# A hybrid encoder layer on one core: the edge columns of group two's row tiles are written by an entry of the convolution's queue

## The chip, the cores and the metric

The kernel runs on one core of one Trainium2 chip. The core has five engines that work side by side, each through its own list of instructions in order, and that wait for one another on semaphores: TensorE (PE in the profile; its weight loads stand as PEld), VectorE (DVE), ScalarE (ACT), GpSimd (POOL) and SyncE (SP), which here only issues transfers. The metric is device time of one execution, in microseconds (us), lower is better. Each kernel is executed several times and the median is compared.

## The reference

One layer of an encoder on two groups of requests, 1024 rows and 256 rows, with shared weights:

```python
hn = rms_norm(x, norm_g)
proj = hn @ w_in
xbc, z_ssd, dt_raw, q, k, v, z_att, mq, z_mem = split_cols(proj, IN_SIZES)
xbc = jax.nn.silu(centred_dwconv(xbc, conv_w, conv_b))
xs, Bm, Cm = split_cols(xbc, (SSD_WIDTH, SSD_GROUPS * SSD_STATE, SSD_GROUPS * SSD_STATE))
```

`xs`, `Bm` and `Cm` feed a state-space scan in both directions, `q`, `k`, `v` an attention in a window of 128 rows, `mq` an attention on a memory of 256 rows. The three results are gated, joined and multiplied by `w_out`, and `x` is added.

The part that matters here is the convolution: each of the 1536 channels of `xbc` is convolved along the rows with five taps centred on the row (two rows to each side, zeros outside the request), a bias is added and SiLU taken. A block of rows therefore needs two rows from each neighbour, and where a request begins or ends it needs zeros.

## The kernel before

**Rows and channels.** The 1280 rows (1024 of the first request, then 256 of the second) are worked on in two groups of 640. For `xbc` the product is laid with channels on the 128 partitions and rows along the free axis, so that the convolution runs along the free axis. There are 12 such tiles of channels for each group. All products are in fp32 as three passes (high by high, low by high, high by low halves). A weight tile is loaded by SP (`wraw`), its high half is copied by ACT (`wh`, L206) and its low half subtracted by DVE (`wl`, L207); the two are called a split below.

**Group one** gets its `xbc` in the stretch before 500 us by another path (`ev_seven`). While it does so, it keeps the last four input columns of each channel tile in `carry` (L361).

**Group two** gets its `xbc` in six blocks, x0 to x5, in the stretch from 590 to 816 us. `block_feat` makes one block: 8 weight tiles, two tiles of channels (the pair), two halves of 320 rows, four accumulators in PSUM of the five in the pool `acc`. For each weight tile but the seventh it runs the matmuls; the seventh's are run with the eighth's. Behind the last matmul of the first channel tile comes its evacuation, behind the last one of the second its own. A block has 192 matmuls of 320 columns (L293, L294, L295), and 16 places (yields) at which other work is let in: two behind each of the first six weight tiles, four behind the eighth, after the first evacuation and ahead of the second.

**The row tile.** The evacuation of group two, the function `f` in `ev_conv` (L388), takes a tile `u` of 650 columns from the two buffers of tag `evu`. Columns 4 to 323 and 324 to 387 are the rest of the first request, 392 to 647 the second request; ACT copies these from PSUM (L394, L395, L396). The edge columns are written by DVE: 0 to 3 from `carry` (L391), 388 to 391 and 648 to 649 with zeros (L392, L393). The evacuation stands in a block of raised priority (`tc.high_priority(offset=HP[1])`, 100): the scheduler that lays each engine's instructions in order may place them earlier than where the program calls them. In the trace the edges of the first tile start at 601.54 us and its copies on ACT at 615.55.

**The queue of the convolution.** When the second tile of a pair is evacuated, `conv_two` makes a list of entries that is put into the queue `left`; one entry is taken at each of the 16 places of the next block (`one_left`, which calls `some_left`). An entry's instructions are put behind the latest weight split on ACT and DVE (`issue_after(marks)`), at ordinary priority. For one tile the entries are `first_tap` (ACT, L357, takes a `c` of tag `evt`, two buffers), four taps (DVE, L362), `silu` (ACT, L365), `last` (DVE, L368, which writes the finished rows into `u`; then SP stores them in two transfers, L372 and L373, into `xbc_d`). `conv_two` overlaps the two tiles by two entries, so a pair has 12. Behind x5 they run in the places of the block for `k`, `v` and `dt` (`block_tok`, one place behind each of 16 weight tiles, 15 matmuls each).

With 12 entries, the pairs of entries behind weight tiles 1 to 6 are: first tap and tap 1; taps 2 and 3; tap 4 with the second tile's first tap, silu with its tap 1; last, and its tap 2; its taps 3 and 4; its silu and its last. The four places behind the eighth weight tile are empty.

**What runs beside it.** At the same 16 places, `pump` takes steps of two more lists of work: the attentions (`attn`, `mem_attn`) and the scan (`ssd_up`). They use PSUM from a pool of three banks (`mix`). In `attn`, `scores` has TensorE write a score tile `psc` (L689, L690) that DVE reads (L691).

Of the kernel before, what the change touches and what calls it, by code (L numbers as in the profile page):

```python
# [44 lines left out]
def hymba_encoder_kernel(  # L45
# [7 lines left out]
    V, A, G, T, S = nc.vector, nc.scalar, nc.gpsimd, nc.tensor, nc.sync  # L53
# [23 lines left out]
    def const(shape, name, dtype=F32):  # L77
        return cp.tile(shape, dtype, tag=name, name=name)
# [22 lines left out]
    carry = const([P, 12, 4], "carry")  # L101
# [239 lines left out]
    left = deque()  # L341
# [7 lines left out]
    def conv_work(grp, fc, u):  # L349

        n = 646 if grp else 638
        cw = [vec[:, R_CW + k * 12 + fc:R_CW + k * 12 + fc + 1] for k in range(5)]
        c = []

        def first_tap():
            c.append(ev.tile([P, 650], F32, tag="evt", name="c")[:, :n])
            A.activation(c[0], u[:, :n], AF.Identity, scale=cw[0], bias=vec[:, R_CB + fc:R_CB + fc + 1])  # L357

        def tap(k):
            if grp == 0 and k == 2:  # L360
                V.tensor_copy(carry[:, fc, :], u[:, 638:642])  # L361
            V.scalar_tensor_tensor(out=c[0], in0=u[:, k:k + n], scalar=cw[k], in1=c[0], op0=ALU.mult, op1=ALU.add)  # L362

        def silu():
            A.activation(u[:, :n], c[0], AF.Tanh)  # L365

        def last():
            V.scalar_tensor_tensor(out=u[:, :n], in0=u[:, :n], scalar=1.0, in1=c[0], op0=ALU.add, op1=ALU.mult)  # L368
            if grp == 0:
                S.dma_start(xbc_d[fc, :, 0:638], u[:, :638])  # L370
            else:
                S.dma_start(xbc_d[fc, :, 638:1024], u[:, :386])  # L372
                S.dma_start(xbc_d[fc, :, 1024:1280], u[:, 390:646])  # L373
        return [first_tap] + [lambda k=k: tap(k) for k in range(1, 5)] + [silu, last]

    def conv_two(a, b):

        def both(f, g):
            def h():
                f()  # L380
                g()
            return h
        return a[:4] + [both(a[4], b[0]), both(a[5], b[1]), a[6]] + b[2:]

    def ev_conv(grp, f0):
        us = []

        def f(fc, ps):  # L388
            fc = f0 + fc
            u = ev.tile([P, 650], F32, tag="evu", name="u")  # L390
            V.tensor_copy(u[:, 0:4], carry[:, fc, :])  # L391
            V.memset(u[:, 388:392], 0.0)  # L392
            V.memset(u[:, 648:650], 0.0)  # L393
            A.activation(u[:, 4:324], ps[0][:, :320], AF.Copy)  # L394
            A.activation(u[:, 324:388], ps[1][:, :64], AF.Copy)  # L395
            A.activation(u[:, 392:648], ps[1][:, 64:320], AF.Copy)  # L396
            us.append(u)
            if len(us) == 2:
                left.extend(conv_two(*[conv_work(grp, f0 + i, us[i]) for i in range(2)]))
        return f  # L400

# [1257 lines left out]
    for b in range(6):  # L1659
        feat("x", b, ev_conv(1, 2 * b), 1, extra=one_left)  # L1660
# [120 lines left out]
```

## Time and profile before

| | |
|---|---|
| median of three runs | 1777.37 us (1776.67 to 1778.53) |
| the profiled execution | 1777.93 us, span from its first to its last instruction 1776.2 us |
| busy in the span: PE, PEld | 1763.4 us (99%), 1608.4 us (91%) |
| DVE, ACT, POOL | 1245.6 us (70%), 918.9 us (52%), 554.6 us (31%) |
| blocks x0 to x5, starts of the first matmuls | 590.2, 621.2, 658.0, 696.2, 735.9, 774.5 us |
| edge instructions L391, L392, L393 | 12 of each, 0.166, 0.062, 0.060 us (medians) |
| DVE idle in front of L391 | 4.9 us in all, 4 times, until stores into `xbc_d` landed |

An engine's busy time leaves out its waits. A wait is put down to the semaphore that came last. A start is counted from the first instruction of the span. Line numbers are those of the kernel before.

### The profile page before, as it was taken

Reading aid. Unit: us, or ns where it says so; the run is one execution under the profiler, and the core shown is the slowest. Engines: PE = TensorE matmul, PEld = TensorE weight load, DVE = VectorE, ACT = ScalarE, POOL = GpSimd, SP = SyncE. Lnnn points to the kernel's source line nnn. Section 1 sums busy time; section 2 is a strip of 40 time slices with the busy share of each in tenths; the row PEclk is TensorE's granted clock in tenths of the full one; section 3 lists DMA queues with packets and bytes.
Section 4 is the critical chain, followed back from the end, with each engine's and each line's share of the span. In section 5 each row is a group of like instructions: output and inputs, shape, how many; then the busy total and the mean of one; then the engine's idle time right before and its main releaser. Section 6 shows DMA issues by size and latency. Waiting matters only on the chain. (4 is left out here: it accounts for less than half of the span.)

```text
span 1776.2 us, 31998 instructions
## 1 busy us (share of the span) xinstructions
PE 1763.4 (99%) x11046; PEld 1608.4 (91%) x11046; DVE 1245.6 (70%) x2348; ACT 918.9 (52%) x2049; POOL 554.6 (31%) x980
## 2 busy tenths in 40 slices
PE   9999999999999999999999999999999999999999
PEld 7888999999998999999889988888988888899999
DVE  5595788888858878777765676557777654766665
ACT  5554555555434766656454565545446633543332
POOL 0105798998810100001000100011110000058775
PEclk9999999999999999999999999999999999999999
DMA  8653444445447544453635645557787854644442
GB/s 293 200 184 115 146 149 147 141 145 168 122 138 213 189 138 134 148 169 99 193 116 187 186 157 156 168 167 249 220 247 233 254 189 145 219 146 146 146 143 78
DMA packets 208210, 301.16 MB, mean 170 GB/s; under 512 B 19568, under 2 KB 86192, under 8 KB 208048
## 3 DMA queue, kind: packets, MB, share of 16 engines
q1 hardware_dynamic: 207904, 299.06, 54.5%
q8 instruction: 87, 1.43, 0.3%
q14 instruction: 75, 0.61, 0.1%
q10 hardware_dynamic: 144, 0.06, 0.0%
HBM read 236.36 MB, written 62.69 MB: 168 GB/s over the span
## 5 line engine op out<-in xcount | busy, mean ns | idle before, releaser
L207 DVE TENSOR_TENSOR wl<-wraw,wh 128x512 fp32r<-128x512 f32 (+1 forms) x480 | 346.7, 724 | 227.6 <-ACT wh L206 218.7
L206 ACT ACTIVATE wh<-wraw 128x512 fp32r<-128x512 f32 (+1 forms) x480 | 292.2, 613 | 294.3 <-PE acc L260 155.8
L258 PE MATMUL acc<-wh,xH 128*128 128x512 f32 (+1 forms) x1088 | 418.5, 385 | 0.6 <-DVE v_all L337 0.3
L260 PE MATMUL acc<-wh,xL 128*128 128x512 f32 (+1 forms) x1088 | 410.2, 377 | 0.0
L259 PE MATMUL acc<-wl,xH 128*128 128x512 f32 (+1 forms) x1088 | 409.8, 377 | 0.1
L258 PEld LDWEIGHTS acc<-wh,xH 128*128 128x128 f32 x1088 | 204.1, 188 | 37.6 <-issue 2.7
L260 PEld LDWEIGHTS acc<-wh,xL 128*128 128x128 f32 x1088 | 204.2, 188 | 36.8 <-issue 0.2
L259 PEld LDWEIGHTS acc<-wl,xH 128*128 128x128 f32 x1088 | 204.4, 188 | 35.7 <-issue 1.2
L293 PE MATMUL acc<-xH,wh 128*128 128x320 f32 x640 | 202.8, 317 | 0.0
L206 ACT ACTIVATE sh<-ws 128x384 fp32r<-128x384 f32 x176 | 91.3, 523 | 207.6 <-POOL ws L1256 109.6
L294 PE MATMUL acc<-xL,wh 128*128 128x320 f32 x640 | 198.6, 310 | 0.0
L295 PE MATMUL acc<-xH,wl 128*128 128x320 f32 x640 | 198.4, 310 | 0.0
L207 DVE TENSOR_TENSOR sl<-ws,sh 128x384 fp32r<-128x384 f32 x176 | 124.9, 713 | 98.1 <-ACT sh L206 94.5
L1256 POOL TENSOR_TENSOR ws<-wraw 128x128 f32<-128x128 f32 x176 | 112.9, 641 | 206.4 <-DMA wraw<-in_w_in_pairs_dram 86.3
L293 PEld LDWEIGHTS acc<-xH,wh 128*128 128x128 f32 x640 | 120.1, 188 | 2.6 <-issue 2.1
L294 PEld LDWEIGHTS acc<-xL,wh 128*128 128x128 f32 x640 | 120.2, 188 | 1.5 <-issue 1.2
L1256 POOL TENSOR_TENSOR ws<-wraw,ws 128x128 f32<-128x128 f32 x176 | 116.7, 663 | 13.8
L295 PEld LDWEIGHTS acc<-xH,wl 128*128 128x128 f32 x640 | 120.2, 188 | 0.7 <-issue 0.7
L1256 POOL TENSOR_TENSOR ws<-ws,wraw 128x128 f32<-128x128 f32 x176 | 118.2, 672 | 0.0
L1256 POOL TENSOR_TENSOR wraw<-wraw 128x128 f32<-128x128 f32 x176 | 111.6, 634 | 13.7
L635 POOL MEMSET lgw<- 128x1 f32 x40 | 3.9, 98 | 313.8 <-DVE lg L698 188.1
L362 DVE SCALAR_TENSOR_TENSOR c<-u,vec,c 128x638 f32<-128x638 f32 (+1 forms) x96 | 90.0, 939 | 9.9 <-ACT c L357 9.5
(440 smaller groups left out, 3954.1 us busy)
## 6 DMA issues: line engine op xcount, KB each, us to landing
wraw<-in_w_in_laid_dram SPq DMA_DIRECT2D x176, 256.0 KB, 2.9
wraw<-in_w_in_pairs_dram SPq DMA_DIRECT2D x112, 256.0 KB, 2.7
wraw<-in_w_out_laid_dram SPq DMA_DIRECT2D x64, 256.0 KB, 3.5
wraw<-in_w_out_pairs_dram SPq DMA_DIRECT2D x64, 256.0 KB, 2.7
rf<-ac SPq DMA_DIRECT2D x40, 256.0 KB, 4.1
rb<-ac SPq DMA_DIRECT2D x40, 256.0 KB, 4.7
wraw<-in_w_mem_laid_dram SPq DMA_DIRECT2D x32, 256.0 KB, 4.5
xst<-in_x_sample_dram SPq DMA_DIRECT2D x20, 256.0 KB, 5.0
```

What stands on the lines that cost most here:

```text
L206: a = A.activation(h, raw, AF.Copy)
L207: b = V.tensor_sub(l, raw, h.bitcast(F32))
L258: T.matmul(ps[t][:, :n], sh, h[:, :n], start=(k_ == 0), stop=False)
L259: T.matmul(ps[t][:, :n], sh, l[:, :n], start=False, stop=False)
L260: T.matmul(ps[t][:, :n], sl, h[:, :n], start=False, stop=(k_ == KT - 1))
L293: T.matmul(o, sh, cur["H", q][:, m, c], start=(k == 0), stop=False)
L294: T.matmul(o, sh, cur["L", q][:, m, c], start=False, stop=False)
L295: T.matmul(o, sl, cur["H", q][:, m, c], start=False, stop=(k == KT - 1))
L362: V.scalar_tensor_tensor(out=c[0], in0=u[:, k:k + n], scalar=cw[k], in1=c[0], op0=ALU.mult, op1=ALU.add)
L635: G.memset(w.bitcast(F32)[(slice(None),) + tuple(slice(n - 1, n) for n in shape)], 0.0)
L1256: G.tensor_tensor(out=o, in0=x, in1=y, op=op)
```

## The change

The three instructions that write a row tile's edge columns leave the evacuation and become a function `edges`. A new first entry of the queue calls it for both tiles of the pair; the entries of `conv_two` follow. A pair now has 13 entries for the 16 places. The instructions themselves, their number and their engine stay.

```diff
+    def edges(fc, u):
+        V.tensor_copy(u[:, 0:4], carry[:, fc, :])
+        V.memset(u[:, 388:392], 0.0)
+        V.memset(u[:, 648:650], 0.0)
+
     def ev_conv(grp, f0):
         us = []
 
         def f(fc, ps):
             fc = f0 + fc
             u = ev.tile([P, 650], F32, tag="evu", name="u")
-            V.tensor_copy(u[:, 0:4], carry[:, fc, :])
-            V.memset(u[:, 388:392], 0.0)
-            V.memset(u[:, 648:650], 0.0)
             A.activation(u[:, 4:324], ps[0][:, :320], AF.Copy)
             A.activation(u[:, 324:388], ps[1][:, :64], AF.Copy)
             A.activation(u[:, 392:648], ps[1][:, 64:320], AF.Copy)
             us.append(u)
             if len(us) == 2:
+                left.append(lambda: [edges(f0 + i, us[i]) for i in range(2)])
                 left.extend(conv_two(*[conv_work(grp, f0 + i, us[i]) for i in range(2)]))
         return f
```

## Prediction

> **What bounds the kernel.** I read the page's first lines, then PE's list of waits over the whole execution (us in total, times, longest), then the busy times of each engine block by block through the six convolution blocks (590 to 816 us) and the block behind them.
>
> ```profile
> span 1776.2 us, 31998 instructions
> PE 1763.4 (99%) x11046; PEld 1608.4 (91%) x11046; DVE 1245.6 (70%) x2348; ACT 918.9 (52%) x2049; POOL 554.6 (31%) x980
> ```
> ```profile
> PE pst L914 <- ACT fh L928: 1.6, 1, 1.6
> ...
> PE psc L689 <- DVE nm L691: 1.4, 1, 1.4
> PE pmt L628 <- DVE mpr L805: 1.4, 1, 1.4
> ```
> ```profile
> core 0: us, PE busy (x) PEld busy (x) DVE busy (x) ACT busy (x) POOL busy (x), PEclk, DMA share, GB/s
> 657.00:695.00 38.00, 36.58 (x263) 34.91 (x262) 31.55 (x67) 26.70 (x68) 4.89 (x10) 1.00 0.49 149
> ...
> 816.00:862.00 46.00, 44.59 (x340) 42.97 (x340) 36.51 (x81) 32.80 (x89) 6.48 (x9) 1.00 0.58 163
> ```
> TensorE sets the end: it is idle for 1776.2 − 1763.4 = 12.8 us in all, at the full granted clock (1.00). No wait on a transfer stands among its longest. In the stretch that the change touches it stands still twice: 38.00 − 36.58 = 1.42 us in block x2, 46.00 − 44.59 = 1.41 us behind the last block. The change moves no matmul, so it can win only what these two cost, and it can lose where it makes DVE, ACT or SP late enough that PE's cover is gone.
>
> The wait in x2 is where the change acts. First DVE, then SP's queue, then PE around it, then ACT at the second evacuation (start in us, duration, engine and line, tiles):
>
> ```profile
> 678.68 0.83 DVE L368 SCALAR_TENSOR_TENSOR u<-u,c 128x646 f32<-128x646 f32 x1 [0.91 <-ACT u L365]
> 679.43 0.68 DVE L207 TENSOR_TENSOR wl<-wraw,wh 128x512 fp32r<-128x512 f32 x1
> 682.17 0.17 DVE L391 COPY u<-carry 128x4 f32<-128x4 f32 x1 [2.06 <-DMA xbc_d<-u]
> ...
> 682.30 0.61 DVE L691 CUSTOM_DVE_ANT_0 lg<-pdist,psc,nsink 128x384 f32<-128x384 bf16 x1
> 682.84 0.69 DVE L207 TENSOR_TENSOR wl<-wraw,wh 128x512 fp32r<-128x512 f32 x1
> ...
> 689.29 0.69 DVE L207 TENSOR_TENSOR wl<-wraw,wh 128x512 fp32r<-128x512 f32 x1
> ```
> ```profile
> 679.54 0.32 SPq L372 DMA_DIRECT2D xbc_d<-u  x1
> 679.91 0.42 SPq L373 DMA_DIRECT2D xbc_d<-u  x1
> ```
> ```profile
> 680.20 0.34 PE L689 MATMUL psc<-kT,qT 128*128 128x384 f32 x1
> ...
> 681.07 0.34 PE L690 MATMUL psc<-kL,qT 128*128 128x384 f32 x1
> 682.98 0.44 PE L689 MATMUL psc<-kT,qT 128*128 128x384 f32 x1 [1.42 <-DVE nm L691]
> ```
> ```profile
> 695.06 0.44 ACT L394 ACTIVATE u<-acc 128x320 f32<-128x320 f32 x1 [0.83 <-PE acc L295]
> ...
> 734.55 0.41 ACT L394 ACTIVATE u<-acc 128x320 f32<-128x320 f32 x1
> ...
> 773.65 0.44 ACT L394 ACTIVATE u<-acc 128x320 f32<-128x320 f32 x1 [0.83 <-PE acc L295]
> ```
> At 678.68 the `last` of block x1's second tile (L368), one of the queue's entries that run in block x2, finishes that row tile, and SP stores it in two transfers. The next thing in DVE's order but one is the edge copy (L391) of a new tile in the same buffer. It waits 2.06 us for the stores to land, and L691, behind it in DVE's order, can't read the first score. PE has written three score pairs by 681.41 and has three `mix` banks, so the fourth stands until L691 is through (682.30 + 0.61 = 682.91), and starts at 682.98. The new tile's own evacuation (L394 of the last fence, by block x2, x3, x4) comes only at 695.06: the edges are 13 us early.
>
> **The change, part by part.** The 36 instructions (three for each of 12 tiles) stay as many, on the same engine.
>
> ```profile
> L391 DVE COPY u<-carry x12: 151/166/171, 601.5 to 798.0; 128x4 f32<-128x4 f32 x12
> L392 DVE MEMSET u<- x12: 62/62/62, 601.7 to 798.1; 128x4 f32 x12
> L393 DVE MEMSET u<- x12: 60/60/60, 601.7 to 798.1; 128x2 f32 x12
> ```
> ```profile
> DVE wl L207 <- ACT wh L206: 23.5, 17, 4.3
> DVE u L391 <- DMA xbc_d<-u: 4.9, 4, 2.1
> ```
> (1) Their work is 12 × (0.166 + 0.062 + 0.060) = 3.5 us at most, off PE's path, where DVE waits 23.5 us for weight halves alone. Moved: 0 on the sum. Without that cover it would still be 0.29 us a tile.
>
> (2) The early place goes, and with it the four waits at the head of DVE's queue, 4.9 us. Three of them reached no PE wait; the one of 2.06 us cost 1.42. Without it DVE is free at 679.43 + 0.68 = 680.11, the first score pair is written by about 680.7, and L691 ends near 681.4, when PE is done with its third pair. **−1.42 us.** What is late next there is nothing: PE stands behind its own third pair. No transfer holds PE later, so it carries to the end.
>
> ```profile
> L373 SPq DMA_DIRECT2D xbc_d<-u x12: 422/424/621, 627.3 to 850.5; - x12
> DMA to landing us min/median/max: 1.9/2.6/4.6
> ```
> (3) The new place: the edges come behind the first weight split of the next block, as step 0. For x2's pair that is behind the split at 689.29. The buffer's previous store is now issued later (part 4): behind the split at 682.84 at the earliest, 682.84 + 0.69 + 0.83 + 0.32 + 0.42 + 2.6 (the median landing) = 687.7. So there the wait is gone, not moved: 0. `first_tap` on ACT now needs DVE's edges: 0.1 to 0.3 us on a chain that has until the block's end. 0.
>
> (4) Twelve entries become thirteen over sixteen steps. Every tap comes one step later; the thirteenth, the second tile's `last` with its two stores, goes from step 11 (behind the sixth weight tile) to step 12, behind the seventh and eighth tiles and the block's first evacuation. Its buffer is the one that the block's second evacuation (L394 on ACT) writes, so that must now wait for stores that are issued some 7 us later. Block x4 has the least room:
>
> ```profile
> 723.03 0.68 DVE L207 TENSOR_TENSOR wl<-wraw,wh 128x512 fp32r<-128x512 f32 x1
> ...
> 753.76 0.69 DVE L207 TENSOR_TENSOR wl<-wraw,wh 128x512 fp32r<-128x512 f32 x1
> ...
> 761.38 0.82 DVE L368 SCALAR_TENSOR_TENSOR u<-u,c 128x646 f32<-128x646 f32 x1
> ...
> 765.78 0.68 DVE L207 TENSOR_TENSOR wl<-wraw,wh 128x512 fp32r<-128x512 f32 x1
> ...
> 769.72 0.68 DVE L207 TENSOR_TENSOR wl<-wraw,wh 128x512 fp32r<-128x512 f32 x1
> ```
> The eighth split of x4 is at 765.78; 0.68 + 0.83 + 0.32 + 0.42 + 2.6 more gives 770.6, 3.0 us ahead of L394 at 773.65. In x2 the same sum (687.7) is 7.4 us ahead of 695.06, in x3 (723.03 + 4.85 = 727.9) 6.7 ahead of 734.55. **0** is my value, since each is ahead; the lower end is 0 (a later store frees nothing earlier), the upper is the slower rival's 3.2 us.
>
> (5) Behind the last block, one step is only 15 matmuls. There `last` at 849.26 stands in DVE's order ahead of the softmax weights that PE waits 1.41 us for:
>
> ```profile
> 849.26 0.84 DVE L368 SCALAR_TENSOR_TENSOR u<-u,c 128x646 f32<-128x646 f32 x1
> ...
> 851.19 0.62 DVE L805 TENSOR_SCALAR mpr<-mpr,mden 128x256 f32<-128x256 f32 x2
> ```
> One step later it may fall behind L805 (at best −1.41) or other taps may fall ahead of it (another of its kind at 0.84: +0.84). I take 0, between the two, as the trace doesn't show which.
>
> **Sum.** The profiled execution took 1777.93 us (span 1776.2 and 1.7 around it). 1777.93 − 1.42 = 1776.5; the median of the runs is 0.56 lower at 1777.37, which gives 1775.95, called **1776.0 us**.
>
> [...]
>
> ```profile
> 773.60 0.31 PE L294 MATMUL acc<-xL,wh 128*128 128x320 f32 x1
> 773.75 0.31 PE L295 MATMUL acc<-xH,wl 128*128 128x320 f32 x1
> ...
> 774.53 0.38 PE L293 MATMUL acc<-xH,wh 128*128 128x320 f32 x1
> ```
>
> **The rivals.**
> A. *Nothing to measure, the wait moves.* The edges still write a buffer whose stores must have landed. In x5 they stand behind the first split, which ran at 769.72, against a landing of 770.6 or later: DVE stands again. If scores or softmax weights stand behind it, as in x2, PE pays 1.4 us again: 1777.4 us. For it: the store moved by as much as the edges did. Against it: of four such waits only one reached PE.
>
> B. *Slower: the second evacuation waits for the late store.* In x4 it decides once DVE reaches `last` more than 3.0 us behind the eighth split. In the trace of before `last` ran 761.38 − 753.76 − 0.69 = 6.9 us behind its own split. With that, the stores land at 777.5; L394 ends at 777.95. The next block's fourth accumulator needs its bank 15 matmuls of 0.15 us after 774.53, at 776.8: 1.2 us of PE, and 3.2 with the longest landing (4.6). ACT stands too, and the weight halves behind it. With no gain from part 2 (DVE's wait moved as in A) that is 1777.4 + 1.2 to 3.2 = 1778.6 to 1780.6; in two blocks with ACT's delay reaching the weights, about 1782. Against it: x2 and x3 have over 6 us of room. [...]
> C. *Both PE waits go:* −1.42 − 1.41, 1774.5 us. For it: one 0.84 us instruction may leave the second wait's way. Against it: other moved taps may take its place.
>
> **How the numbers follow.** Forecast 0.45, A 0.27, B 0.18, C 0.10. About 0.2%, 3.55 us, is what a measurement of this kernel can tell from no change: 1773.8 to 1780.9. The forecast and A lie inside nearly whole (0.01 and 0.02 lost by other order of DVE's work); of B about half lies above (0.09), of C 0.05 below. So faster 0.06, same 0.83, slower 0.11. The range goes down to both waits gone and the 0.7 us by which the lowest run is under the median (1773.8), and up to B in one block with a landing between median and longest, 1780.0.
>
> **What would show it.** Right: L391 to L393 start behind each block's first split, within 1 us ahead of L357, and no L689 waits for L691 in x2; PE's waits from 590 to 816 us come to under 0.3 us. Part 4 shows in L368's second tile starting behind the eighth split and in what ended ACT's idle time before L394: PE if I am right, the store if B is. Rival A shows as DVE waiting in front of L391 with PE's waits still at 1.4 us. Wrong is the forecast if the time is over 1778 with no new PE wait in these blocks, or if the 1.42 us are gone and the time is not lower.

## The result and the profile after

| | before | after |
|---|---|---|
| median | 1777.42 us (22 runs, 1775.31 to 1781.84) | 1774.78 us (22 runs, 1773.26 to 1779.7) |
| the profiled execution | 1777.93 us, span 1776.2 us | 1773.26 us, span 1771.5 us |

The ratio is 0.9985, with a 95% interval of 0.9979 to 0.999: 2.64 us less, 0.15%. That is less than the 0.2% called measurable, though the interval doesn't reach 1; it is inside the range, and 1.2 us under the forecast. In the kernel after the line numbers are higher: the score tile's L689 to L691 became L692 to L694, L394 became L396, L805 became L808, and the edges are L386 to L388.

The page of after, first lines, and PE's waits over its whole execution (us in total, times, longest):

```profile
span 1771.5 us, 32002 instructions
...
PE 1762.3 (99%) x11046; PEld 1608.5 (91%) x11046; DVE 1245.5 (70%) x2348; ACT 918.9 (52%) x2049; POOL 550.5 (31%) x980
```
```profile
...
PE pmt L631 <- DVE mpr L808: 0.6, 1, 0.6
...
```
PE, DVE, ACT and POOL run as many instructions as before, and the first three are busy as long to 0.1%. The row of PE's wait for `nm` in block x2 is gone, and the wait for `mpr` behind the last block is 0.6 us instead of 1.4. By stretch, first before, then after (columns as in the prediction: us, then busy time of PE, PEld, DVE, ACT, POOL, the granted clock, the DMA share, GB/s):

```profile
590.00:880.00 290.00, 287.17 (x2149) 274.36 (x2148) 223.79 (x507) 183.63 (x462) 27.25 (x60) 1.00 0.50 151
```
```profile
590.00:880.00 290.00, 289.16 (x2164) 276.07 (x2163) 227.06 (x514) 184.78 (x465) 26.75 (x60) 1.00 0.51 152
...
657.00:695.00 38.00, 38.00 (x278) 36.59 (x277) 32.35 (x70) 28.33 (x72) 4.46 (x10) 1.00 0.52 155
...
811.00:857.00 46.00, 45.40 (x344) 44.05 (x343) 37.66 (x81) 33.29 (x90) 5.87 (x9) 1.00 0.55 160
```
In block x2 PE is now busy for 38.00 of 38.00 us (36.58 before); behind the last block it idles 0.60 us (1.41 before).

Two profiled executions also differ in places where the programs don't: the spans differ by 4.7 us, more than the medians do. So I counted progress by matmuls. Both programs run the same 8,880 matmuls into accumulators; numbered from 0 by their start, the time from one number to another is compared. Number 3900 starts in block x2 ahead of the place of the old wait, 3961 behind it, 4780 shortly ahead of the wait for `mpr`, 4908 in the next block:

| us between the starts of matmuls | 3900 to 3961 (x2) | 3961 to 4780 (x2 to x5 and on) | 4780 to 4908 (behind the last block) |
|---|---|---|---|
| before; before again | 12.77; 12.92 | 164.98; 164.97 | 34.41; 34.85 |
| after; after again | 11.22; 11.22 | 164.67; 164.66 | 33.73; 33.84 |

After less before is −1.55 −0.31 −0.68 = −2.54 us in the one pair of profiles and −1.70 −0.30 −1.01 = −3.01 in the other, against −2.64 of the medians. So the gain has two main places: x2, and the block behind the last one. The 0.3 us between them is spread over the blocks, without a wait of PE that went; it is not traced further here.

DVE in x2 after:

```profile
679.47 0.61 DVE L694 CUSTOM_DVE_ANT_0 lg<-pdist,psc,nsink 128x384 f32<-128x384 bf16 x1 [1.01 <-PE psc L693]
...
680.01 0.69 DVE L207 TENSOR_TENSOR wl<-wraw,wh 128x512 fp32r<-128x512 f32 x1
...
687.72 0.81 DVE L368 SCALAR_TENSOR_TENSOR u<-u,c 128x646 f32<-128x646 f32 x1
...
689.75 0.15 DVE L386 COPY u<-carry 128x4 f32<-128x4 f32 x1
...
691.72 0.17 DVE L386 COPY u<-carry 128x4 f32<-128x4 f32 x1 [0.47 <-DMA xbc_d<-u]
...
722.56 0.82 DVE L368 SCALAR_TENSOR_TENSOR u<-u,c 128x646 f32<-128x646 f32 x1
...
763.75 0.83 DVE L368 SCALAR_TENSOR_TENSOR u<-u,c 128x646 f32<-128x646 f32 x1
```
```profile
688.93 0.45 SPq L373 DMA_DIRECT2D xbc_d<-u  x1
```
```profile
692.20 0.44 ACT L396 ACTIVATE u<-acc 128x320 f32<-128x320 f32 x1 [0.34 <-PE acc L295]
...
731.67 0.41 ACT L396 ACTIVATE u<-acc 128x320 f32<-128x320 f32 x1
...
770.69 0.44 ACT L396 ACTIVATE u<-acc 128x320 f32<-128x320 f32 x1 [0.83 <-PE acc L295]
```
The score reads now run straight through the place where DVE stood for 2.06 us. The edges come at 689.75 and 691.72; the second tile's still wait 0.47 us for the store, and nothing of PE waits behind them. The second tile's `last`, at 687.72, is 7.0 us behind the end of its split (680.01 + 0.69), because score reads and softmax instructions of the attention, steps of the scan and the next block's first split stand ahead of it. Its second store was issued at 688.93 and had landed by 691.72, 0.5 us ahead of the second evacuation at 692.20, which waited for PE alone.

### The profile page after: what moved, and what is told of

Its sections match the earlier page's. It is cut to its first block, busy times and chain, and to the rows that moved or that the text cites. A ratio compares the mean times of both kernels' runs of the same rounds, so it can differ in the third digit from the quotient of the medians.

```text
span 1771.5 us, 32002 instructions
## 1 busy us (share of the span) xinstructions
PE 1762.3 (99%) x11046; PEld 1608.5 (91%) x11046; DVE 1245.5 (70%) x2348; ACT 918.9 (52%) x2049; POOL 550.5 (31%) x980
## 3 DMA queue, kind: packets, MB, share of 16 engines
q8 instruction: 87, 1.43, 0.3%
```

## The experiments

Two questions were open. In x2: is the edges' early place the cause of PE's wait, or the order of DVE's work in general? Behind the last block: why is the wait for `mpr` shorter? Each kernel was compared with the kernel before on the same chip. No kernel leaves any of the computation out. Progress by matmuls, as above, for those without a disturbance of the clock there (further down):

| kernel | x2 | x2 to x5 and on | behind the last block | ratio to before (95%) |
|---|---|---|---|---|
| empty entry | 11.22 | 164.75 | 34.21 | 0.9994 (0.9985 to 1.0003) |
| one tile | 11.21 | 165.01 | 34.83 | 0.9995 (0.9986 to 1.0004) |
| edges on GpSimd | 11.21 | 164.99 | 34.12 | 0.9994 (0.9985 to 1.0003) |
| late stores | 11.21 | 167.98 | 34.35 | 1.0015 (1.0006 to 1.0024) |
| early load, in before | 12.11 | 165.00 | 33.81 | 0.9998 (0.9989 to 1.0007) |
| early load, in after | 11.22 | 164.66 | 33.52 | 0.9986 (0.9978 to 0.9995) |
| last held back | 12.94 | 164.95 | 34.38 | 1.0 (0.9991 to 1.0009) |

### The two kernels once more

> The kernel before, unchanged, for a second profile. Every theory expects the time of before within 0.5 us, and the two PE waits that the change took part in, 1.42 us in block x2 (the score tile behind L691, with DVE idle 2 us in front of L391) and 1.41 us behind the last block (behind L805). If the first is not there again, or is under 0.7 us, then what I took for the cause was an accident of one execution. The waits at 150 us (1.4 us, ACT behind a load) and near 1339 us (1.6 us) lie where the two programs have the same order; they are expected to differ between executions by as much as they did between the two kernels (0.7 us).

> The changed kernel, unchanged, for a second profile and more runs: 2.6 us faster than before. PE's wait in x2 is gone again in every theory. The wait behind the last block was 1.41 and 1.6 us in two profiles of before, 1.4 to 1.6 in the runs with the edges at the first tap or with the empty entry, and 0.6 in the changed kernel. If the change itself shortens it (theory 3), it is 0.6 again, within 0.2 us. If 0.6 came from the landing of one load (ACT waited 0.5 us for the memory queries there, against 1.3 to 1.4 in the others), it is anywhere between 0.6 and 1.6.

Before again: 1776.98 us against 1777.28, ratio 0.9998 (0.9989 to 1.0007). After again: 1775.31 against 1777.07, 0.999 (0.9981 to 0.9999). PE's waits from 580 to 870 us, before again and then after again:

```profile
PE psc L689 <- DVE nm L691: 1.6, 1, 1.6
PE pmt L628 <- DVE mpr L805: 1.6, 1, 1.6
...
```
```profile
PE pmt L631 <- DVE mpr L808: 0.9, 1, 0.9
```
Both waits of before and the one of after come back at nearly their sizes, so they belong to the programs and not to one execution.

### Edges together with the first tap (twelve entries)

```diff
-                left.append(lambda: [edges(f0 + i, us[i]) for i in range(2)])
-                left.extend(conv_two(...))
+                work = conv_two(...)
+                first = work[0]
+                left.append(lambda: ([edges(f0 + i, us[i]) for i in range(2)], first()))
+                left.extend(work[1:])
```

> The edges leave the evacuation as in the change, but run in the same entry as the first tap, so that a pair has 12 entries as before and no tap and no store comes later. Theory 1 (the early place of the edges was the cost): 1.4 us faster than before, PE's wait in x2 gone, PE's wait behind the last block still 1.4 us. Theory 2 (the later steps are what gains): same time as before within 0.4 us. Theory 3 (both parts add): 1.4 us faster here, and the rest of the 2.6 us in the run with the empty entry.

1775.34 us against 1777.28, ratio 0.9994 (0.9985 to 1.0003). No wait for `psc` is left, the x2 piece is 11.22 us, and DVE waits for no store. PE's waits from 820 to 870 us:

```profile
PE pmt L633 <- DVE mpr L810: 1.9, 2, 1.6
```
The late place of the edges alone, with no step shifted, takes all of the wait in x2 and nothing of the one for `mpr`.

### An empty first entry (edges where they were)

```diff
-                left.extend(conv_two(*[conv_work(grp, f0 + i, us[i]) for i in range(2)]))
+                left.append(lambda: None); left.extend(conv_two(*[conv_work(grp, f0 + i, us[i]) for i in range(2)]))
```

> The kernel before with an empty entry at the head of the queue: edges in the evacuation as before, 13 entries, every tap and the second tile's stores one step later. Theory 1: no gain (within 0.4 us of before), since the edges still wait in front of L691 in x2 or wherever the later store puts them; the sum of DVE's waits in front of L391 grows over 4.9 us, as the stores come later. Theory 2: 2.6 us faster. Theory 3: 0.8 to 1.2 us faster, with PE's wait behind the last block at 0.6 us and PE's wait in x2 unchanged at 1.4 us.

1775.97 us against 1777.28. PE's waits from 580 to 870 us, then DVE's for the stores in the same time:

```profile
PE pmt L628 <- DVE mpr L805: 1.4, 1, 1.4
PE psc L689 <- DVE nm L691: 0.3, 1, 0.3
```
```profile
DVE u L391 <- DMA xbc_d<-u: 3.3, 3, 1.9
```
The expectation that the shift of one step alone would change nothing fell: the x2 piece is 11.22 us here too, and the 0.3 us left stand in block x1, at 635.41 us. DVE still stands for stores, three times and 3.3 us in all, but no longer with the score reads behind it. So PE's wait was a coincidence of two things, and either edit breaks it: the edges at the head of DVE's queue, and the place of the store relative to the scores.

### Four buffers for the row tile

```diff
-            u = ev.tile([P, 650], F32, tag="evu", name="u")
+            u = rp.tile([P, 650], F32, tag="ch", name="u", bufs=CH)
```

> The kernel before with the row tiles of group two in the four buffers of tag ch, which no other work uses in these blocks, in place of the two of tag evu: the edges stay early but find a buffer whose stores landed long ago. 12 entries. Theory 1: DVE doesn't wait in front of L391, PE's wait in x2 is gone, 1.4 us faster than before. Theory 2: same as before within 0.4 us. If DVE's waits go and the time stays, the wait in x2 was not worth its 1.4 us.

1778.31 us against 1777.28, ratio 1.001 (1.0001 to 1.0019). DVE in block x2, then PE's waits:

```profile
683.71 0.17 DVE L391 COPY u<-carry 128x4 f32<-128x4 f32 x1 [2.75 <-DMA xbc_d<-u]
```
```profile
PE psc L689 <- DVE nm L691: 1.9, 1, 1.9
```
More buffers were expected to take the wait away. They didn't: the copy at 683.71 belongs to a tile that is evacuated only one block later. The first four edge copies, one for each buffer, now all run between 603 and 611 us, ahead of x0's evacuations. So the scheduler has put the raised edges about as early as a buffer is free, and with two buffers more it is a later tile's edges that stand behind the same store. What has to change is their place, not the room. (Why the median is 1 us higher is taken up in the last section.)

### One tile's edges alone

Only the three instructions for the second tile of x2 (the sixth tile of channels) move, into the first tap's entry of their pair; every other instruction keeps its order.

```diff
+            if fc != 5:
+                edges(fc, u)
...
+                if fc == 5:
+                    work[0] = lambda g=work[0]: (edges(fc, u), g())
```

> The kernel before, but the edges of one tile of twelve (the second of block x2) are written in the entry of its pair's first tap; the other eleven stay in the evacuation. 12 entries, and every engine but DVE has the order of before; on DVE these three instructions alone move. Theory 1 (the one wait in x2 is what PE paid): 1.4 to 1.6 us faster, as much as with all twelve moved; DVE's waits in front of L391 fall by 2.1 us and the other three stay. Theory 2 (later steps): the time of before within 0.4 us.

1776.44 us against 1777.07. PE's waits and DVE's for stores, 580 to 870 us:

```profile
PE pmt L635 <- DVE mpr L812: 1.6, 1, 1.6
```
```profile
DVE u L386 <- DMA xbc_d<-u: 4.3, 4, 1.7
```
Three instructions of 0.29 us together account for the whole wait in x2: its piece is 11.21 us. The other tiles still wait, for 4.3 us in all, at no cost to PE. The ratio, 0.9995 (0.9986 to 1.0004), can't tell 1.5 us from nothing; what decides is the trace.

### Edges on GpSimd

```diff
-            V.tensor_copy(u[:, 0:4], carry[:, fc, :])
-            V.memset(u[:, 388:392], 0.0)
-            V.memset(u[:, 648:650], 0.0)
+            G.tensor_copy(u[:, 0:4], carry[:, fc, :])
+            G.memset(u[:, 388:392], 0.0)
+            G.memset(u[:, 648:650], 0.0)
```

> The kernel before with the three edge instructions on GpSimd, still in the evacuation and early, 12 entries. The wait for the stores then stands at the head of GpSimd's queue. Theory 1: PE's wait in x2 is gone, 1.4 us faster, as long as nothing that PE waits for stands behind the edges on GpSimd; if GpSimd's own instructions for the attention stand behind them, part of the 1.4 us is paid back by DVE's waits for it (up to 2 us). Theory 2: the time of before.

1775.65 us against 1777.07. The waits of GpSimd for the stores, 580 to 870 us:

```profile
POOL u L391 <- DMA xbc_d<-u: 43.9, 8, 18.1
```
The same early place, the same stores, and 43.9 us of standing, at no cost to PE, whose x2 piece is 11.21 us. Here the wait was harmful only for what stood behind it on its engine.

### Later stores

The changed kernel, with two more stores of each pair's second tile, into an array that nothing reads: extra work ahead of the second evacuation.

```diff
+                if fc % 2:
+                    for _ in range(2):
+                        S.dma_start(idle_d, u)
```

> The changed kernel with two more stores of each pair's second row tile (into a scratch array that nobody reads) behind its two. The buffer comes free some 2 to 4 us later. Rival B, the second evacuation's wait for these stores: in the changed kernel the last store of x1's second tile was issued at 688.93 and the evacuation ran at 692.20, so in x2 ACT must now wait 2 to 4 us in front of L396, and PE 0.5 to 2.5 us for its accumulator; in x4 0 to 1 us. That would make it 0.5 to 3.5 us slower than the changed kernel. If the cover is as I put it (7.4 us in x2, 3.0 in x4), only x4 can show a wait, under 1 us, and the time is that of the changed kernel within 0.5 us.

1780.29 us against 1777.07, ratio 1.0015 (1.0006 to 1.0024): 5 us more than after again in the same comparison, and more than the 0.5 to 3.5 us expected; 3.3 us of it lie between x2 and x5 (167.98 against 164.66). ACT's and PE's waits, 580 to 870 us, then ACT's evacuations and DVE in x4:

```profile
ACT u L400 <- DMA idle_d<-u: 5.2, 2, 3.4
```
```profile
PE acc L294 <- ACT u L400: 1.6, 1, 1.6
PE pmt L635 <- DVE mpr L812: 1.4, 1, 1.4
PE psc L696 <- DVE nm L698: 1.3, 1, 1.3
```
```profile
699.79 0.44 ACT L400 ACTIVATE u<-acc 128x320 f32<-128x320 f32 x1 [1.80 <-DMA idle_d<-u]
...
776.64 0.44 ACT L400 ACTIVATE u<-acc 128x320 f32<-128x320 f32 x1 [3.36 <-DMA idle_d<-u]
```
```profile
776.60 0.17 DVE L390 COPY u<-carry 128x4 f32<-128x4 f32 x1 [2.58 <-DMA idle_d<-u]
```
This is rival B made to happen. The second evacuation waits 1.80 us in x2 and 3.36 us in x4, and PE pays 1.6 us at the first (its matmul at 700.28 waits for L400). The mechanism is real; in the changed kernel it stayed away by 0.5 us in x2. The 1.3 us of scores in x4 belong to rival A as well: the next pair's edges wait 2.58 us for the same store on DVE, DVE works without a pause from there, and the scores are read behind that, at 780.76. Which of the two waits PE paid for there, this run doesn't separate.

### The memory tile's load earlier, in before and in after

Across the profiles one more number moves with PE's wait for `mpr`: how long ACT stands ahead of `mqh` for the load of a memory tile (`mq<-mT`) some 16 us earlier. Before, first ACT, then DVE:

```profile
835.48 0.63 ACT L775 ACTIVATE mqh<-mq 128x512 fp32r<-128x512 f32 x1 [1.32 <-DMA mq<-mT]
```
```profile
838.24 0.46 DVE L207 TENSOR_TENSOR wl<-wraw,wh 128x288 fp32r<-128x288 f32 x1 [1.00 <-ACT wh L206]
```
After, ACT:

```profile
831.54 0.63 ACT L778 ACTIVATE mqh<-mq 128x512 fp32r<-128x512 f32 x1 [0.51 <-DMA mq<-mT]
```
ACT waits 1.32 us, its next weight half is late, DVE waits 1.00 us for it, and from there works without a pause up to L805, on which PE waits 1.41 us. After, 0.51 and 0.60; after again, 0.78 and 0.89; before again, 1.49 and 1.57; empty entry, 1.42 and 1.41. It isn't bound to one version: in the later stores, which are the changed kernel, ACT waits 1.43 us and PE 1.42. The five other profiles without an early load have ACT at 1.26 to 2.01 and PE's wait at 1.32 to 1.64. The edit moves one transfer forward on SP's queue, past six others in before and seven in after; no other instruction on any engine changes its order:

```diff
         turn_(0)
+        if t == 0:
+            fetch_next()
         yield
...
         values(0)
-        fetch_next()
+        if t != 0:
+            fetch_next()
```

> The kernel before with one transfer moved: SyncE issues the load of the second memory tile (mq<-mT) seven instructions earlier, ahead of another weight load; the order of every other instruction on every engine is the same, and no work is left out. Theory 3 (the wait behind the last block is passed on from that load): ScalarE stands for it 1.32 us, its next weight half is late, VectorE's work behind that is late, and PE's wait for mpr follows at the same size (1.32 and 1.41 us before, 1.49 and 1.57 before again, 0.51 and 0.60 after, 0.78 and 0.89 after again). It expects ScalarE's wait in front of mqh to be under 0.2 us, PE's wait for mpr under 0.3, the stretch of block x2 as long as before (12.8 us), and some 1.2 to 1.4 us less: 0.9992 of before. The rival (VectorE has too much work there, whatever the load) expects ScalarE's wait gone, PE's wait still 1.4 us and no change of time.

> The changed kernel with the same one transfer moved earlier on SyncE's queue; nothing else differs from it and no work is left out. Theory 3: PE's wait for mpr goes from 0.6 to 0.9 us to under 0.3, the time is 0.5 to 0.9 us under that of after: 1774.0, ratio 0.998 to before, and the gain of early_load over before is larger than that of this kernel over after by 0.5 to 0.8 us. The rival (VectorE has too much work) expects PE's wait at 0.6 to 0.9 us and 1774.8.

In before: 1776.46 us against 1777.5, ratio 0.9998 (0.9989 to 1.0007). In after: 1774.62, ratio 0.9986 (0.9978 to 0.9995). ACT no longer stands for this load in either. PE's waits, 580 to 900 us, early load in before and then in after:

```profile
PE psc L689 <- DVE nm L691: 0.8, 1, 0.8
PE pmt L628 <- DVE mpr L805: 0.5, 1, 0.5
PE pmo L827 <- ACT mpT L816: 0.4, 1, 0.4
```
```profile
PE pmt L631 <- DVE mpr L808: 0.4, 1, 0.4
PE pmo L830 <- ACT mpT L819: 0.3, 1, 0.3
```
The load's landing is the larger part of the cause: with one transfer moved the wait falls from 1.4 to 1.6 us to 0.5, and the piece behind the last block from 34.41 or 34.85 to 33.81 us, as far as the change itself brought it. The expected "under 0.3" was not reached: 0.4 to 0.5 stay. The wait of 0.3 to 0.4 us for `mpT` behind it is not this edit's doing: before again has it too, at 0.38 us, and after at 0.24. In after there is so little left (33.73 or 33.84 to 33.52) that the time doesn't show it; the two versions can't be told apart. In before the wait for `psc` was 0.8 us in this execution with the same order of DVE's instructions; DVE stood 1.74 us for the store there, instead of 2.06, so the size of PE's wait varies from one execution to the next. The ratio of this kernel shows no gain by itself; the reading rests on the trace.

### The last entry held back

```diff
-RATES[1]["kv"], extra=lambda k: some_left() if left else None)
+RATES[1]["kv"], extra=lambda k: some_left() if left and (len(left) > 1 or k == 15) else None)
```

> The kernel before, where the last entry of the queue behind the last block (the second tile's last, 0.84 us on VectorE, and its two stores) is held back to the block's last step, so that it stands behind the softmax weights (mpr) that PE waits for, not ahead of them; no work is left out. The prediction's part 5 took this for the way in which the wait could go: by its 0.84 us, PE's wait falls from 1.41 to some 0.6 us, and the time by 0.8. Theory 3 expects less: the softmax weights also need ScalarE's exponentials, which ended at 850.40 us of the profile before, against 850.99 where VectorE turned to them, so at most 0.5 us of the wait goes, and ScalarE still stands 1.3 us for the load.

1776.95 us against 1777.5, ratio 1.0 (0.9991 to 1.0009). PE's waits, then DVE at the softmax weights:

```profile
PE pmt L628 <- DVE mpr L805: 1.3, 1, 1.3
```
```profile
850.79 0.17 DVE L801 RECIPROCAL mden<-mden 128x2 f32<-128x2 f32 x1 [0.26 <-ACT mpr L799]
850.99 0.61 DVE L805 TENSOR_SCALAR mpr<-mpr,mden 128x256 f32<-128x256 f32 x2
```
With 0.84 us of work out of its way, L805 starts only 0.2 us earlier (850.99 against 851.19): DVE now waits for ACT's exponentials. PE's wait is shorter by 0.1 us, and the piece behind the last block as long as before, 34.38 us. The order of `last` and L805 was not what set this wait.

## Why the prediction was right, and where it was not

The change was called too small to tell, under 0.2%, and it is 0.15%. The range held it. The forecast named the right main term, but the result lies 1.2 us under it and 0.3 us over rival C's 1774.5, which had a chance of 0.10. C has the time nearly right, not the way: the second wait fell by 0.7 to 0.8 us and didn't go, and `last` did not leave its way.

**What bounds the kernel.** Right. PE set the end, and the gain is what it no longer waits. Before, its matmuls of 320 columns started 0.15 us apart where it ran without a wait (773.60, 773.75), and in x2 it was busy for 36.58 of 38.00 us, 1.42 short, its weight loads for 34.91. x2 gave 1.55 to 1.70 us, and after it PE's matmuls fill 38.00 of 38.00 us while the weight loads stand at 36.59.

**Part 1, the edges' own work.** Right: 0.15 and twice 0.06 us a tile, nothing of PE behind them.

**Part 2, −1.42 us.** Right, and shown three ways: one tile's edges moved, all of them moved with no step shifted, or the same edges on GpSimd each bring the x2 piece to 11.21 or 11.22 us. What the prediction didn't see is that part 4's shift of one step would by itself have done the same, so the wait was less firm than it looked.

**Part 3, no wait in the new place.** Off by 0.47 us on DVE, 0 on the sum as forecast. The store was taken to land at 687.7; it landed near 691.7. Rival A was right that a wait stays on DVE (for x2's pair, where A named x4's) and wrong that PE pays for it in this kernel: right behind it stood two weight halves and a tap, and scores only 2.2 us later.

**Part 4, 0 for the later stores.** The value was right, its margins were not. The sum set `last` directly behind its split; in x2 seven us of score reads and softmax work came between, and 7.4 us of room were 0.5. In x3 and x4 the same sum from the rows of after gives 722.56 + 0.82 + 0.32 + 0.42 + 2.6 = 726.7 against 731.67, and 763.75 + 0.83 + 0.32 + 0.42 + 2.6 = 767.9 against 770.69: 5.0 and 2.8 us of room where 6.7 and 3.0 were forecast. The tightest block was x2, which the prediction took for the one with the most room. The later stores show what 0.5 us kept away: a ratio over 1, in part by rival A's wait.

**Part 5, 0 behind the last block.** This is the term that was mis-sized: it measured −0.68 and −1.01 us. The step that failed is that the wait was read only from DVE's last instructions ahead of it (`last` before or behind L805). `last` stayed ahead of L805 after, and holding it back in before shortened the wait by 0.1 us only. What decided was a load 16 us earlier: the chain is SP's load, ACT's wait, a weight half, DVE's backlog, PE. Before, the load was issued at 830.69 and took 4.8 us to land; after, at 828.27, and took 3.2 us (3.5 in after again). SP's queue and the row of the transfers (KB each, median us to landing) of before, then of after:

```profile
830.21 0.42 SPq L899 DMA_DIRECT2D rf<-ac  x1
830.69 0.53 SPq L496 DMA_DIRECT2D mq<-mT  x1
...
mq<-mT SPq DMA_DIRECT2D x1, 256.0 KB, 4.8
```
```profile
826.70 0.33 SPq L902 DMA_DIRECT2D rf<-ac  x1
827.89 0.33 SPq L213 DMA_DIRECT2D wraw<-in_w_in_laid_dram  x1
828.27 0.53 SPq L499 DMA_DIRECT2D mq<-mT  x1
...
mq<-mT SPq DMA_DIRECT2D x1, 256.0 KB, 3.2
```
In both, three loads are issued close together: before, `rf`, `mq` and, 0.63 us behind it, `wraw`; after, `rf`, `wraw` and `mq`, over a longer time. What made the landing quicker stays open. The order and the spacing of the three don't settle it: in the later stores they are those of after to 0.02 us, and the load took 4.2 us. Neither edit alone brought the quick landing: 4.8 us with the empty entry, 4.4 with the late edges, and PE's wait stayed at 1.4 and 1.6 us. Why it takes both together is open too.

## What to carry to other kernels

In this kernel an engine's wait cost what stood behind it in that engine's order: 2.06 us of DVE ahead of the score reads cost PE 1.42 us, 43.9 us of GpSimd cost it nothing. So ask of each early instruction which buffer it needs, which transfer frees that buffer and what is queued behind; moving it to another engine or behind the urgent work took PE's wait in x2 away, while with four buffers 1.88 us of it stood. When the room ahead of a late transfer is worked out, count the work that is already queued on the engine that has to produce the data, not only the step at which it is let in: in x2 that made 7.4 us of room 0.5. And follow a wait back past the engine that is named: a load that took 4.8 us to land, not 3.2, came before a wait of PE of 1.41 us, not 0.60, some 16 us later.

## What the hardware showed that was not expected

Behind some waits of PE the granted clock fell. In three of the profiles its mean over the execution was under 1.000: 0.998 (edges with the first tap), 0.997 (four buffers) and 0.999 (later stores); in the ten others it was 1.000. In four buffers it was 0.51 for 3.40 us shortly behind the wait for `psc` of 1.88 us, and 0.50 for 3.40 us (856.3 to 859.7) shortly behind the wait of 1.6 us for `mpr`. With the edges at the first tap it was 0.66 over the 5.00 us from 853 to 858, behind PE's two waits for `mpr` (1.9 us together, the longer 1.6). Where it fell in the later stores no view here shows. Four buffers, by stretch around the wait for `psc` (columns as above):

```profile
682.60:684.40 1.80, 0.05 (x1) 0.00 (x0) 0.69 (x6) 0.00 (x0) 0.00 (x0) 1.00 0.42 143
684.40:685.60 1.20, 1.07 (x7) 1.08 (x8) 1.20 (x6) 0.71 (x2) 0.00 (x0) 1.00 0.03 7
685.60:689.00 3.40, 3.40 (x15) 3.40 (x15) 3.40 (x14) 1.91 (x6) 0.10 (x1) 0.51 0.24 77
689.00:692.00 3.00, 3.00 (x22) 2.80 (x22) 1.12 (x4) 1.86 (x4) 0.10 (x1) 0.99 0.00 0
```
At half the clock, 3.4 us hold 1.7 us of work, so by this estimate such a dip costs up to 1.7 us on top of the wait; the stretch from matmul 3961 to 4780, which holds the one behind `psc`, took 166.52 us against 164.98 in before, 1.54 us more. Waits of 1.4 to 1.6 us in the profiles with a mean of 1.000 had no such dip behind them (before 1.4, 1.4 and 1.6, before again 1.6 and 1.6), and one of 1.6 us in four buffers did, so the length alone doesn't decide. That a wait brings the dip about is the author's reading of their order; no run shows it apart from what else ran there.

The mean granted clock that stands on record for every execution points the same way for those whose trace is not kept. By the estimate above, one such dip takes 3.4 × 0.5 / 1776 = 0.001 off the mean; so one in four buffers, one with the edges at the first tap and the one in the later stores stand in the mean alone. Of the 29 executions of before next to the early load, 18 had 1.000 and a median of 1776.40 us, 11 had 0.999 and a median of 1779.32. With four buffers 6 of 11 were below 1.000; the other 5 have a median of 1776.78 us against 1776.90 of before at 1.000, so that kernel's extra 1 us seems to lie in its share of such executions. Which waits they fell behind is not shown. The kernel before has more waits near that length than the one after (1.6, 1.4 and 1.4 us in its profile where after has 0.9, 0.6 and none); of its executions in the three comparisons 25 of 95 were below 1.000, of the changed kernel's 5 of 33, too few to say that it meets more dips.
